# Fillers in the opening, weight splits moved to VectorE, adaLN columns in the up stage, and slack for TensorE's operands in the plan

## The chip, the cores and the metric

The kernel runs on one NeuronCore of a Trainium2 chip. The metric is the device time of one execution of the program in microseconds. The kernel before takes 800.14 us, the median of 3 runs (799.01, 800.98 and 800.14). One more execution was profiled; it took 800.93 us.

A NeuronCore has TensorE (matrix products, PE in the profile), VectorE (DVE), ScalarE (ACT), GpSimd (POOL) and SyncE (SP, which here only issues DMAs). Each has its own queue of instructions; they meet through semaphores. Matmuls read their operands from SBUF and write to PSUM banks.

## The reference, cut to what matters

One block of an encoder for a sequence of S = 512 with D = 1024, all in float32. Its parts, in the order of the reference:

```python
mod = silu(c) @ w_ada + b_ada                      # six vectors of 1024
h = rms_norm(x, norm1_g) * (1 + scale1) + shift1
qa, ka, va, qb, kb, vb, qi, ki, wi, gates = split(h @ w_in)   # 512 x (6 x 512 + 324 + 2048)
y_a = dsa_sparse_attention(rms_norm(qa), rms_norm(ka), va, qi, ki, wi)   # top 128 keys a query
y_b = differential_attention(rms_norm(qb), rms_norm(kb), vb, lam)        # two softmaxes, subtracted
merged = g_a * (y_a @ w_up_a) + g_b * (y_b @ w_up_b)          # g = sigmoid(gates)
x = x + gate1 * (merged @ w_o)
h2 = rms_norm(x, norm2_g) * (1 + scale2) + shift2
ff = (silu(h2 @ w_ff1) * (h2 @ w_ff3)) @ w_ff2                # inner width 2816
x = x + gate2 * ff
```

Both attentions are causal by chunks of 64 and have ALiBi distances; the sparse one scores keys with an indexer (qi, ki, wi) and keeps the 128 best.

## The kernel before, in words

**Precision.** Every float32 operand of a matmul is written as a high and a low half in the type fp32r: ScalarE casts (`whi<-raw`, line 429), and VectorE (`wlo<-raw,whi`, line 453) or GpSimd (the same name, line 501) subtracts the cast from the value. A product is three matmuls, high by high, high by low and low by high, summed in a PSUM bank (`three`, line 516 in the trace). The subtraction is called a split below. The set `ON_DVE` names the kinds of weights whose split VectorE does; before, these are the first eight blocks and the feed-forward part's, and GpSimd does the rest.

**Weights.** They come in blocks ("units") of 128 x 1024, half a megabyte each, in the order in which the stages need them: eight blocks `p` (indexer and branch b's q and k), two blocks a quad of heads (`qb0`, `kb1` and so on), 16 gate units `g0` to `g15`, 8 up units `u0` to `u7`, 8 blocks of the output projection w_o (called `o`, tiles `wo`), then the feed-forward blocks. There are four raw buffers and three buffers each for the halves. SyncE issues the loads in the planned order, and an issue waits for a free raw buffer. The adaLN matrices use the same raw buffers: a column unit of the second norm (`ada_col(1, j)`) is two transfers of `adat`, two column sums of 128 x 1024 on VectorE (line 473, shown as CUSTOM_DVE_ANT_0 and a short read of the accumulator; an ISA row in the order) and two small operations for `acol` and `hcol`. A row of a residual gate (`ada_row`) is one transfer of `adar` and one multiply-add of 128 x 1024 on VectorE (line 467).

**Stages.** The opening loads x, sums its squares, takes the root on GpSimd (`rpow`, line 482), scales the four tiles of x (set `XS`: on ScalarE; the others on VectorE), and transposes 128 columns at a time. Per block of 128 channels it needs two column sums for the first norm; ScalarE then scales and shifts the transposed tile (line 438), casts it (`hh`), and VectorE makes the low half (`hl`). For the first block this is done in four pieces. Six matmuls on ready data (`idle`, line 805) whose result nobody reads stand ahead of the first transposes. From about 62 us on come the indexer's scores (`sc`), the search for the best keys (MAX8 and MATCH_REPLACE8, `select`), the quads with their normalization (`qn`, `qkT`, `qk`), the heads A0 to A7 and B0 to B3 (`S`, `PT`, `PV`), the gates between them, the eight up units (a product with the sigmoid of a gate for either branch, their sum, and the cast and split `mh`, `ml`), the output projection with the residual, the second norm, and from 440 us on the feed-forward part.

**What sets the order.** Operations are not issued where they are written. A class `Order` records each with its engine, an estimated cost, its buffers, and a priority: its number in the recording, shifted where the code stands in `moved(d)` (a negative shift is earlier). `plan` then runs a list scheduler over all engines: at each point in planned time an engine takes, of the operations whose inputs are done, the one with the lowest priority that has its buffers. An input is done at the planned end of its maker plus a latency from the table `HOPS`, by pair of engines. The order so found is the program, and each engine then works through its queue in that order, with the real times. The string `PROG` gives the recording's order between opening and output projection: quads and heads by name, `s8` eight rounds of the search, `g` and `u` the units, and `l2` two of the late adaLN items, eight rows and then eight column units of the second norm. Weight blocks are recorded ahead of their use with a shift of −250.

## Time and profile before

| | |
|---|---|
| time, median of 3 runs | 800.14 us |
| profiled execution | 800.93 us |
| its span, first to last instruction | 799.1 us |
| mean granted clock of TensorE | 0.996 |
| busy share PE, DVE, ACT, POOL | 98%, 57%, 44%, 25% |
| read from HBM | 95.16 MB |

The profile shows one execution. The span is its time from the first to the last instruction; 1.8 us lie around it. Busy time counts an engine's work without waiting, issuing or branching. A row of a timeline gives start, duration, engine, line, operation, the tiles written and read, and in brackets how long the engine stood idle before, and what ended that. [...] Matmuls overlap, so a row's duration is longer than its distance to the next one.

### The profile page before, as it was taken

What the parts mean: (1) busy time and instruction counts of PE and PEld (TensorE: products, weight loads), DVE (VectorE), ACT (ScalarE), POOL (GpSimd) and SP (SyncE); (2) the same over time, 40 slices, a digit from 0 to 9 for tenths busy, and PEclk for the clock granted to TensorE, in tenths of its full rate; (3) what the DMA queues carried; (4) which work ended last, traced back from release to release, by engine and by line L of the source; (5) the groups of instructions that cost most, each with busy time, mean ns of one, the idle gap of its engine ahead of it and who ended that gap; (6) DMA issues with size and microseconds to landing.
All of it is one profiled execution on the core that took longest, in us unless ns stands there. A gap on an engine that the chain in (4) does not pass through costs nothing.

```text
span 799.1 us, 11091 instructions
## 1 busy us (share of the span) xinstructions
PE 781.9 (98%) x4261; PEld 673.9 (84%) x4261; DVE 456.2 (57%) x898; ACT 350.1 (44%) x649; POOL 200.3 (25%) x129
## 2 busy tenths in 40 slices
...
GB/s 348 398 136 53 81 69 65 80 80 65 83 107 117 106 55 87 149 185 279 168 237 80 80 106 112 129 154 153 138 105 85 101 106 84 100 106 85 126 40 66
DMA packets 29147, 97.97 MB, mean 123 GB/s; under 512 B 3235, under 2 KB 4771, under 8 KB 29094
## 3 DMA queue, kind: packets, MB, share of 16 engines
...
q14 instruction: 20, 0.16, 0.1%
HBM read 95.16 MB, written 2.10 MB: 122 GB/s over the span
## 4 chain that ended last, share of the span: by engine, by line
PE 85%; DVE 7%; issue 3%; DMA 2%; ACT 2%; POOL 1%; SPq 0%; POOLq 0%; ACTq 0%; DVEq 0%
PE ff L516 44%; PE gate L516 11%; PE up L516 5%; PE wo L516 3%; PE kb L516 3%; PE qa L516 3%; PE ka L516 2%; PE S L516 2%; PE PT L529 2%; PE qb L516 2%; PE idx L516 2%; PE PVa L516 1%; PE va L516 1%; PE vb L516 1%; DMA raw<-in_wun 1%
## 5 line engine op out<-in xcount | busy, mean ns | idle before, releaser
L429 ACT CAST whi<-raw 128x1024 fp32r<-128x1024 f32 x109 | 114.6, 1052 | 292.3 <-PE ff L516 148.2
L501 POOL TENSOR_TENSOR wlo<-raw,whi 128x1024 fp32r<-128x1024 f32 x46 | 114.9, 2499 | 157.9 <-ACT whi L429 133.3
L453 DVE TENSOR_TENSOR wlo<-raw,whi 128x1024 fp32r<-128x1024 f32 x63 | 77.1, 1225 | 117.4 <-ACT whi L429 114.6
L516 PE MATMUL ff<-h2l,whi 128*128 128x512 f32 (+1 forms) x384 | 142.5, 371 | 0.0
L516 PE MATMUL ff<-h2h,wlo 128*128 128x512 f32 (+1 forms) x384 | 142.4, 371 | 0.0
L516 PE MATMUL ff<-h2h,whi 128*128 128x512 f32 (+1 forms) x384 | 142.3, 372 | 0.0
L516 PE MATMUL ff<-whi,f 128*128 128x512 f32 (+1 forms) x310 | 95.1, 385 | 0.0
L516 PEld LDWEIGHTS ff<-h2l,whi 128*128 128x128 f32 x384 | 72.3, 188 | 12.5
L516 PEld LDWEIGHTS ff<-h2h,wlo 128*128 128x128 f32 x384 | 72.2, 188 | 12.5
L516 PEld LDWEIGHTS ff<-h2h,whi 128*128 128x128 f32 x384 | 72.2, 188 | 12.5
L516 PEld LDWEIGHTS ff<-whi,f 128*128 128x128 f32 x310 | 58.0, 188 | 11.6
L516 PE MATMUL ff<-wlo,f 128*128 128x512 f32 (+1 forms) x155 | 59.5, 385 | 0.0
L459 DVE TENSOR_TENSOR silu<-ff,silu 128x512 f32<-128x512 f32 x22 | 15.2, 692 | 69.4 <-PE ff L516 69.4
L516 PE MATMUL gate<-hh,whi 128*128 128x512 f32 x128 | 51.4, 402 | 0.0
L516 PE MATMUL gate<-hh,wlo 128*128 128x512 f32 x128 | 51.1, 401 | 0.0
L516 PE MATMUL gate<-hl,whi 128*128 128x512 f32 x128 | 51.0, 399 | 0.0
L473 DVE CUSTOM_DVE_ANT_0 raw<-raw,cs 128x1024 f32<-128x1024 f32 x32 | 45.7, 1440 | 4.2 <-DMA raw<-in_adat 2.7
L438 ACT ACTIVATE sx<-sx,nm 128x128 f32<-128x128 f32 (+3 forms) x64 | 35.7, 560 | 9.7 <-DVE nm L473 9.4
L482 POOL TENSOR_TENSOR r<-v,mhalf 128x16 f32<-128x16 f32 (+2 forms) x14 | 27.9, 1993 | 43.9 <-DVE v L463 40.3
L516 PEld LDWEIGHTS ff<-wlo,f 128*128 128x128 f32 x155 | 29.1, 188 | 5.9
L467 DVE SCALAR_TENSOR_TENSOR acc<-raw,csc,acc 128x1024 f32<-128x1024 f32 x16 | 20.7, 1294 | 22.0 <-DMA raw<-in_adar 21.9
L516 PE MATMUL wo<-wo,mh 128*128 128x512 f32 x96 | 30.2, 393 | 1.3 <-ACT mh L429 1.3
...
## 6 DMA issues: line engine op xcount, KB each, us to landing
raw<-in_wun SPq DMA_DIRECT2D x118, 512.0 KB, 3.3
raw<-in_adat SPq DMA_DIRECT2D x32, 512.0 KB, 7.3
raw<-in_adar SPq DMA_DIRECT2D x16, 512.0 KB, 3.3
x<-in_x SPq DMA_DIRECT2D x4, 512.0 KB, 5.9
...
xr<-in_x SPq DMA_DIRECT2D x4, 512.0 KB, 5.8
...
```

What stands on the lines that cost most here:

```text
L429: nc.scalar.copy(g(o), g(i))
L438: nc.scalar.activation(g(o), g(i), f, scale=g(scale), **kw)
L453: dve(n, False, lambda: nc.vector.tensor_sub(g(o), g(i), g(j)), (i, j), (o,), two=(i, j))
L459: dve(n, False, lambda: nc.vector.tensor_mul(g(o), g(i), g(j)), (i, j), (o,), two=(i, j))
L467: dve(n, False, lambda: nc.vector.scalar_tensor_tensor(g(o), g(i), g(s), g(j), op0=op0, op1=op1), (i, s, j), (o,), len(refs(s)), (i, j))
L473: dve(n, False, lambda: nc.vector.tensor_tensor_reduce(g(o), g(i), g(j), scale, init, op0, op1, g(acc)), (i, j), (o, acc), two=(i, j))
L482: G.op("POOL", 300 + 165 * m, lambda: nc.gpsimd.tensor_tensor(g(o), g(i), g(mhalf[:, 0:1].spread([P, m])), op=ALU.pow), refs(i, mhalf), re ...
L501: G.op("POOL", 147 + 2.106 * n, lambda: nc.gpsimd.tensor_sub(g(o.r()), g(i), g(hi)), (i, hi), (o,), port=True)
L516: lambda: nc.tensor.matmul(g(ap), g(lhsT.r()), g(rhs.r()), start=i == 0, stop=i == self.count - 1), refs(lhsT, rhs), (ap,))
L529: G.op("PE", 109, lambda: nc.tensor.transpose(g(ap), g(in_), g(idt)), refs(in_, idt), (ap,))
```

## The change

There are five edits. (1) The opening has thirteen idle matmuls instead of six. They use a bank of the transposes' pool (`tb`) and stand 60 places later in priority, so that the plan puts them where TensorE has nothing else; they are recorded at a planned cost of 500 instead of 700. Tile 0 of x goes to ScalarE too (`XS`), and the small activation `csc` has to wait for the last cast of the first block's pieces. (2) VectorE instead of GpSimd splits the output projection's blocks, the up units, and seven of the gate units. (3) The second norm's column units leave the list behind `l` and get a letter of their own, `k`; `PROG` spreads the rows from the u0 stage on and one column unit at a time from g7 to u5. (4) `l2` items stand later: none is left between the heads. (5) The plan adds 300 ns to the latency from ScalarE, VectorE or GpSimd to TensorE, so that a matmul counts as ready that much later.

```diff
@@ -37,7 +37,7 @@
 
 
 PROG = """scores s8 g0 qb1 vb0 B1 vb1 B0 g3 qa0 g13 g12 kb1 ka0 s9 s8 s9 B2 va0 s99 s8 qa1 g10 B3 g8 ka1 A2 A0 A3 va1
-A1 l2 A4 A6 l2 g2 g9 g5 A5 l2 A7 u0 g1 l2 u1 g11 g14 g7 g15 u2 u3 l2 l2 g4 g6 l2 u4 u5 u6 u7 l99"""
+A1 A4 A6 g2 g9 g5 A5 A7 u0 l2 g1 u1 l2 g11 g14 l2 g7 k1 l2 g15 k1 u2 k1 u3 k1 g4 k1 g6 k1 u4 k1 u5 k1 u6 u7 l99 k99"""
 PROG = PROG.split()
 
 
@@ -145,13 +145,14 @@
 
 
 W_MOVE, L_MOVE, S_MOVE = 250, -200, -100
-ON_DVE = ('f1', 'f3', 'f2', 'p')
+ON_DVE = ('f1', 'f3', 'f2', 'p', 'o', 'up') + tuple(('g', j) for j in (1, 11, 14, 7, 15, 4, 6))
 NRAW, NW, NT = 4, 3, 36
 DMA_LAG = 2000.0
+PE_SLACK = 300.0
 FS = 2
 DUP_POOL = ('kb0', 'kb1', 'ka0')
 HA = 4, 4, 4, 1
-XS = (1, 2)
+XS = (0, 1, 2)
 ADA_TAG = "pt"
 PC, XE, IB, H_MOVE, GT = 4, 4, 8, 40, 1
 LA = 2
@@ -358,6 +359,8 @@
                 n += 1
                 for d in pick.then:
                     x = pick.end + self.HOPS.get((e, d.eng), self.HOP)
+                    if d.eng == "PE" and e in ("ACT", "DVE", "POOL"):
+                        x += PE_SLACK
                     if x > d.ready:
                         d.ready, d.last = x, pick
                     d.need -= 1
@@ -423,7 +426,7 @@
     def refs(*xs):
         return [x for x in xs if isinstance(x, Ref)]
 
-    def act(o, i, n, f=AF.Copy, bias=None, scale=1.0, accum=None, also=()):
+    def act(o, i, n, f=AF.Copy, bias=None, scale=1.0, accum=None, also=(), after=()):
         def fn():
             if f == AF.Copy and bias is None and not isinstance(scale, Ref) and scale == 1.0:
                 nc.scalar.copy(g(o), g(i))
@@ -439,7 +442,7 @@
         table = f if f in (AF.Exp, AF.Sigmoid, AF.Silu) else None
         k, psum = len(refs(bias, scale, accum)), isinstance(i.v, Bank)
         op = G.op("ACT", (52 if psum else 94) + 0.833 * n + 93 * k, fn, refs(i, bias, scale), refs(o, accum), also=also,
-                  after=exps if f == AF.Sigmoid else (), table=table)
+                  after=exps if f == AF.Sigmoid else after, table=table)
         if f == AF.Exp:
             exps.append(op)
         return op
@@ -492,7 +495,7 @@
         return r
 
     def cp(o, i, n):
-        act(o.r(), i, n)
+        return act(o.r(), i, n)
 
     def sb(o, i, hi, n):
         sub(o.r(), i, hi, n)
@@ -659,8 +662,9 @@
             c = slice(p * n, p * n + n)
             act(f[:, c].k(p), b[:, c].k(p), n, AF.Identity, bias=one(hcol, cb), scale=one(acol, cb))
             h, l = (x[:, cb, c].k((0, p) if cb == 0 else cb) for x in (hh, hl))
-            cp(h, f[:, c].k(p), n)
+            cast = cp(h, f[:, c].k(p), n)
             sb(l, f[:, c].k(p), h, n)
+        return cast
 
     def stat_mm(bank, w, k, c=None, m=128, n0=0, n1=512, key=None):
         c = k * P if c is None else c
@@ -793,19 +797,20 @@
             dma(cst, a["cst"], 266)
             dma(lamv, a["lam"][0].partition_broadcast(P), 128)
             make_gains()
-            act(csc, vec[:, V_CC:V_CC + 8], 8, AF.Silu)
+            act(csc, vec[:, V_CC:V_CC + 8], 8, AF.Silu, after=(cast,))
         w = take(("p", cb))
         if cb == 0:
             scale_x(NB - 1)
         with G.moved(-H_MOVE if cb else 0):
-            make_h(cb)
+            cast = make_h(cb) if cb == 0 else (make_h(cb), cast)[1]
         if cb == 0:
-            idle = Bank("idle")
-            for _ in range(6):
-                G.op("PE", 700, lambda: nc.tensor.matmul(g(idle[:, 0:256]), g(cs[:, 0:P]), g(cs[:, 0:256]), start=True, stop=True),
-                     (cs,), (idle,))
             bi = [Bank("idx", x) for x in ("sb", "sb", "tb")]
             bq, bk = [Bank("qb0"), Bank("qb0")], [Bank("kb0"), Bank("kb0")]
+            idle = Bank("idle", "tb")
+            with G.moved(60):
+                for _ in range(13):
+                    G.op("PE", 500, lambda: nc.tensor.matmul(g(idle[:, 0:256]), g(cs[:, 0:P]), g(cs[:, 0:256]), start=True, stop=True),
+                         (cs,), (idle,))
         def index_mm():
             stat_mm(bi[2], w, cb, c=256, m=68, key=324)
             stat_mm(bi[0], w, cb, c=0, n0=128, key=324)
@@ -1069,7 +1074,7 @@
                     else:
                         select_end(i)
 
-    late = [("r", 0, k) for k in range(8)] + [("c", 1, cb) for cb in range(8)]
+    late, late2 = [("r", 0, k) for k in range(8)], [("c", 1, cb) for cb in range(8)]
     last = [("r", 1, k) for k in range(8)]
 
     def ada_late(n):
@@ -1081,6 +1086,12 @@
                         ada_col(1, j)
                     else:
                         ada_row(s, j)
+
+    def ada_cols(n):
+        for _ in range(n):
+            if late2:
+                with G.moved(L_MOVE):
+                    ada_col(1, late2.pop(0)[2])
 
     ohl = {}
     onum = [0]
@@ -1102,7 +1113,7 @@
             tag = "pt" if i < 4 else ("sx" if i < 7 else "t")
             hi, lo = pair(tag, "wo")
             cp(hi, t[:, kk * 512:kk * 512 + 512], 512)
-            psub(lo, t[:, kk * 512:kk * 512 + 512], hi, 512)
+            (sb if "o" in ON_DVE else psub)(lo, t[:, kk * 512:kk * 512 + 512], hi, 512)
             ohl[2 * k + kk, h] = (hi, lo)
 
     for w in PROG:
@@ -1112,7 +1123,7 @@
             for i in range(1, NB):
                 scores(i)
         else:
-            {"s": select, "A": head_a, "B": head_b, "g": gate, "u": up, "l": ada_late}[w[0]](int(w[1:]))
+            {"s": select, "A": head_a, "B": head_b, "g": gate, "u": up, "l": ada_late, "k": ada_cols}[w[0]](int(w[1:]))
 
 
     ahead(UIX[("o", 3, 1)] + 1)
```

The first place is the start of TensorE's queue. `cs` is the broadcast of the conditioning vector, `xT` are the transposes of x, `qb` and `kb` the first matmuls with a weight. Before, it stands like this:

```order
L601 MATMUL cs<-crow,ones 128x512 x2
L805 MATMUL idle<-cs 128x256 x6
L529 MATMUL xT<-vec,x 128x128 x6
L516 MATMUL qb_204<-whi,hh 128x256
L516 MATMUL qb_204<-wlo,hh 128x256
```

And after the change:

```order
L604 MATMUL cs<-crow,ones 128x512 x2
L812 MATMUL idle<-cs 128x256 x8
L532 MATMUL xT<-vec,x 128x128
L812 MATMUL idle<-cs 128x256 x2
L532 MATMUL xT<-vec,x 128x128
L812 MATMUL idle<-cs 128x256
L532 MATMUL xT<-vec,x 128x128
L812 MATMUL idle<-cs 128x256
L532 MATMUL xT<-vec,x 128x128
L812 MATMUL idle<-cs 128x256
L532 MATMUL xT<-vec,x 128x128 x4
L519 MATMUL qb_217<-whi,hh 128x256
```

Eight idle matmuls stand in a row and five between the first transposes.

The second place is VectorE's queue where the first score tile of the search (`sc`) is summed and the first quads are normalized (`qn`) and stacked (`qk`), with the numbers of the tiles. The old queue has here:

```order
L463 TENSOR_SCALAR sc_784<-relu_772,wi_770 128x256
L467 SCALAR_TENSOR_TENSOR sc_784<-relu_778,wi_770,sc_784 128x256
L467 SCALAR_TENSOR_TENSOR sc_784<-relu_793,wi_770,sc_784 128x256
L459 TENSOR_TENSOR qn_811<-kb0_207,r_762 128x512
L453 TENSOR_TENSOR qk_798<-qkT_781,qk_798 64x512
L453 TENSOR_TENSOR qk_804<-qkT_781,qk_804 64x512
L459 TENSOR_TENSOR qn_840<-kb0_235,r_762 128x512
L467 SCALAR_TENSOR_TENSOR sc_784<-relu_813,wi_770,sc_784 128x256
L866 MEMSET sc_784 64x64
L872 MAX m8_868<-sc_784 128x8
L453 TENSOR_TENSOR qk_850<-qkT_835,qk_850 64x512
L453 TENSOR_TENSOR qk_862<-qkT_835,qk_862 64x512
```

The new one, from the second multiply-add on:

```order
L470 SCALAR_TENSOR_TENSOR sc_798<-relu_806,wi_784,sc_798 128x256
L470 SCALAR_TENSOR_TENSOR sc_798<-relu_812,wi_784,sc_798 128x256
L462 TENSOR_TENSOR qn_828<-kb0_221,r_779 128x512
L456 TENSOR_TENSOR qk_816<-qkT_800,qk_816 64x512
L456 TENSOR_TENSOR qk_825<-qkT_800,qk_825 64x512
L871 MEMSET sc_798 64x64
L877 MAX m8_855<-sc_798 128x8
L878 MATCH_REPLACE sc_798<-m8_855,sc_798 128x256
L462 TENSOR_TENSOR qn_871<-kb0_260,r_779 128x512
L877 MAX m8_884<-sc_798 128x8
L878 MATCH_REPLACE sc_798<-m8_884,sc_798 128x256
L456 TENSOR_TENSOR qk_876<-qkT_857,qk_876 64x512
```

The third multiply-add has moved ahead of the first `qn` of kb, and the search's first two rounds stand ahead of the second pair of `qk` subtractions.

The third place is VectorE's queue at the end of the up stage, where the product of unit 5 and its successors (`gate`), and the output projection's operand (`ml`) are made. Before:

```order
L459 TENSOR_TENSOR gate<-up,gate 128x512 x3
L453 TENSOR_TENSOR ml<-gate,mh 128x512
L459 TENSOR_TENSOR gate<-up,gate 128x512
L456 TENSOR_TENSOR gate<-gate 128x512
L459 TENSOR_TENSOR gate<-up,gate 128x512
L453 TENSOR_TENSOR ml<-gate,mh 128x512
L456 TENSOR_TENSOR gate<-gate 128x512
L453 TENSOR_TENSOR ml<-gate,mh 128x512
L456 TENSOR_TENSOR gate<-gate 128x512
```

And after, from the product of unit 6 on:

```order
L462 TENSOR_TENSOR gate<-up,gate 128x512 x2
L456 TENSOR_TENSOR wlo<-raw,whi 128x1024
L456 TENSOR_TENSOR wo<-raw,wo 128x512 x5
L456 TENSOR_TENSOR ml<-gate,mh 128x512
L456 TENSOR_TENSOR wo<-raw,wo 128x512
L459 TENSOR_TENSOR gate<-gate 128x512
L456 TENSOR_TENSOR wo<-raw,wo 128x512 x6
L456 TENSOR_TENSOR ml<-gate,mh 128x512
L462 TENSOR_TENSOR gate<-up,gate 128x512 x2
L456 TENSOR_TENSOR wlo<-raw,whi 128x1024
L459 TENSOR_TENSOR gate<-gate 128x512
L456 TENSOR_TENSOR ml<-gate,mh 128x512
```

The twelve halves of w_o and two splits of 1024 columns stand between the products of the last two units; the column sums, of which the old queue still had four behind this place, all stand ahead of it.

## Rows read from the trace of the kernel before

**Rows 1.** The head of the page: span, then busy time of each engine, its share of the span and its instructions.

```profile
span 799.1 us, 11091 instructions
...
PE 781.9 (98%) x4261; PEld 673.9 (84%) x4261; DVE 456.2 (57%) x898; ACT 350.1 (44%) x649; POOL 200.3 (25%) x129
```

**Rows 2.** Busy time by stretch: the stretch in us from the span's start and its length, then busy us and instructions of PE, PEld, DVE, ACT and POOL, the granted clock, the DMA engines' share and GB/s.

```profile
62.00:108.00 46.00, 43.13 (x322) 40.37 (x322) 44.28 (x124) 27.18 (x57) 25.45 (x17) 1.00 0.20 70
108.00:310.00 202.00, 200.91 (x1369) 182.84 (x1368) 152.69 (x396) 135.15 (x311) 105.98 (x71) 1.00 0.25 84
310.00:378.00 68.00, 68.00 (x303) 56.35 (x302) 39.60 (x60) 26.00 (x36) 29.33 (x13) 1.00 0.53 181
378.00:395.00 17.00, 14.20 (x60) 10.51 (x58) 11.90 (x11) 9.39 (x17) 15.84 (x10) 1.00 0.56 185
395.00:440.00 45.00, 44.45 (x236) 37.87 (x237) 32.27 (x56) 20.88 (x51) 11.55 (x10) 1.00 0.47 160
440.00:799.00 359.00, 355.33 (x1650) 297.49 (x1648) 130.83 (x145) 94.15 (x116) 0.00 (x0) 1.00 0.31 104
```

**Rows 3.** The same view for two pieces of the opening.

```profile
11.33:14.74 3.41, 1.14 (x7) 0.58 (x6) 2.55 (x8) 1.75 (x3) 1.63 (x1) 1.00 1.04 408
14.74:21.57 6.83, 5.62 (x25) 5.52 (x26) 6.77 (x16) 5.21 (x14) 0.00 (x0) 0.50 1.04 401
```

**Rows 4.** Timeline of TensorE in the opening. The trace counts the six idle matmuls as twelve passes.

```profile
6.25 5.35 PE L805 MATMUL idle<-cs 128*128 128x256 f32 x12
...
15.95 0.58 PE L516 MATMUL qb<-whi,hh 128*128 128x256 f32 x1 [1.32 <-ACT hh L429]
...
18.04 0.41 PE L516 MATMUL qb<-wlo,hh 128*128 128x256 f32 x1
18.25 0.41 PE L516 MATMUL qb<-whi,hl 128*128 128x256 f32 x1
...
24.30 0.28 PE L516 MATMUL qb<-whi,hh 128*128 128x256 f32 x1
24.42 0.28 PE L516 MATMUL qb<-wlo,hh 128*128 128x256 f32 x1
```

**Rows 5.** Timelines of GpSimd, VectorE and ScalarE in the opening: the root, the last step of the first block's shift, the first scaled and shifted piece, and the low half of the second block.

```profile
11.27 1.68 POOL L482 TENSOR_TENSOR r<-v,mhalf 128x2 f32<-128x2 f32 x1 [3.08 <-DVE bs L463]
...
13.67 0.15 DVE L456 TENSOR_TENSOR hcol<-mcol,vec 128x1 f32<-128x1 f32 x1
...
14.92 0.80 ACT L438 ACTIVATE xT<-xT,hcol,acol 128x128 f32<-128x128 f32 x2
...
21.96 0.68 DVE L453 TENSOR_TENSOR hl<-xT,hh 128x512 fp32r<-128x512 f32 x1
```

**Rows 6.** Timelines of TensorE, VectorE and GpSimd around 70 us.

```profile
72.78 0.63 PE L529 MATMUL qkT<-vec,qn 128*128 128x128 f32 x4 [1.76 <-DVE qk L453]
...
68.10 2.46 DVE L467 SCALAR_TENSOR_TENSOR sc<-relu,wi,sc 128x256 f32<-128x256 f32 x1
...
70.78 0.43 DVE L872 MAX8 m<-sc 128x8 f32<-128x256 f32 x1
71.24 1.39 DVE L453 TENSOR_TENSOR qk<-qkT,qk 64x512 fp32r<-64x512 f32 x2
...
67.88 2.40 POOL L501 TENSOR_TENSOR wlo<-raw,whi 128x1024 fp32r<-128x1024 f32 x1 [0.31 <-ACT whi L429]
```

**Rows 7.** Waits of TensorE from 62 to 310 us: what waited, for what, and then us in total, times, longest.

```profile
PE S L516 <- DVE nm L473: 0.9, 2, 0.5
```

**Rows 8.** Groups of instructions over the whole span: count, busy us and mean ns of one, and the idle time before them.

```profile
L501 POOL TENSOR_TENSOR wlo<-raw,whi 128x1024 fp32r<-128x1024 f32 x46 | 114.9, 2499 | 157.9 <-ACT whi L429 133.3
L453 DVE TENSOR_TENSOR wlo<-raw,whi 128x1024 fp32r<-128x1024 f32 x63 | 77.1, 1225 | 117.4 <-ACT whi L429 114.6
...
L473 DVE CUSTOM_DVE_ANT_0 raw<-raw,cs 128x1024 f32<-128x1024 f32 x32 | 45.7, 1440 | 4.2 <-DMA raw<-in_adat 2.7
...
L501 POOL TENSOR_TENSOR wo<-raw,wo 128x512 fp32r<-128x512 f32 x12 | 19.4, 1644 | 1.2 <-ACT wo L429 1.2
```

**Rows 9.** Timeline of TensorE at the start of the output projection.

```profile
384.75 0.50 PE L516 MATMUL wo<-wlo,mh 128*128 128x512 f32 x1 [1.37 <-POOL wlo L501]
...
389.25 0.73 PE L516 MATMUL wo<-wo,mh 128*128 128x512 f32 x2 [1.25 <-ACT mh L429]
```

**Rows 10.** Timelines of VectorE and GpSimd in the up stage: a product and the column sums behind it, and a split of GpSimd's.

```profile
341.04 0.69 DVE L459 TENSOR_TENSOR gate<-up,gate 128x512 f32<-128x512 f32 x1 [17.26 <-PE up L516]
341.64 1.22 DVE L473 CUSTOM_DVE_ANT_0 raw<-raw,cs 128x1024 f32<-128x1024 f32 x1
...
355.58 2.58 POOL L501 TENSOR_TENSOR wlo<-raw,whi 128x1024 fp32r<-128x1024 f32 x1 [2.72 <-ACT whi L429]
...
356.38 2.87 DVE L473 CUSTOM_DVE_ANT_0 raw<-raw,cs 128x1024 f32<-128x1024 f32 x1 [0.47 <-issue]
...
359.18 1.22 DVE L473 CUSTOM_DVE_ANT_0 raw<-raw,cs 128x1024 f32<-128x1024 f32 x1
360.32 0.08 DVE L473 DVE_READ_ACCUMULATOR2_ANT mcol<- 128x1 f32 x1
360.32 0.21 DVE L467 SCALAR_TENSOR_TENSOR acol<-mcol,bs,vec 128x1 f32<-128x1 f32 x1
```

**Rows 11.** DMA issues from 310 to 400 us: count, KB each, median us from issue to landing.

```profile
raw<-in_wun SPq DMA_DIRECT2D x16, 512.0 KB, 3.9
```

## The prediction

> **What bounds the kernel now.** I read the page's head first, then the busy time of each engine stage by stage, then the opening microsecond by microsecond, then TensorE's waits, and last the groups of VectorE and GpSimd. [...] First, TensorE works 781.9 of 799.1 us [rows 1], so only its idle time, its slow clock and the tail after its last matmul can be won. Second, the stretch from 440 us on holds nothing: the feed-forward part is one unbroken row of matmuls, and the 3.67 us that TensorE lacks there (359.00 − 355.33 [rows 2]) are the output's last steps, which the change leaves alone. Third, the losses sit in four places [rows 2]: 62 to 108 us (46.00 − 43.13 = 2.87 idle), 108 to 310 us (202.00 − 200.91 = 1.09), 378 to 395 us (17.00 − 14.20 = 2.80) and 395 to 440 us (0.55). [...]
>
> **The opening.** Before, the six idle matmuls run back to back from 6.25 us and are over at 11.6; the first real matmul starts at 15.95 [rows 4]. The change has thirteen, five of them between the first transposes, each of which waits for its scaled tile of x; so the engine is idle in short pieces, not in one long one. If the clock then stays at its upper level, every 256-column matmul after 15.95 starts 0.12 us after the one before it (24.30 to 24.42) and not 0.21 (18.04 to 18.25) [rows 4]: 5.62 busy us become 5.62 × 0.12/0.21 = 3.2, a gain of 2.4. Not all of it arrives. VectorE now scales the last x tile between the two column sums of the first unit and not behind them, and that waits for GpSimd's root, which ended at 12.95 [rows 5]; I shift the root by −0.25 for the tile that ScalarE now scales, and find scale end 13.4, second sum 14.6, hcol about 15.0 instead of 13.8 [rows 5]. ScalarE's transposed piece started at 14.92 behind its casts before, now at 15.1: the start slips by 0.2. And the second unit's low half (hl), which came at 21.96 + 0.68 = 22.64 [rows 5], still comes at about 22.9, since four pieces of the first unit's are now done behind one more sum; TensorE at full clock is there at about 22.4. So 2.4 − 0.2 − 0.5 = 1.7, and I take 1.5. Ends: 2.4, and −0.3 where the clock falls all the same and only the later start is left. The seven added matmuls cost nothing so long as the last is over before the first real one; eight in a row from 6.25 end near 12.4, the other five fill waits. ScalarE's later csc has no reader before the rows of the first gate.
>
> [...]
>
> **62 to 108 us.** The longest wait is 1.76 us before a transposition (qkT) that needs a PSUM bank [rows 6]. The bank is freed by two subtractions at 71.24 that stand behind a 2.46 us multiply-add, which ended as GpSimd's split (67.88 + 2.40) did [rows 6]; the operation itself takes 0.5. In the new order all three multiply-adds of that sum stand in front of kb's normalization, ahead of GpSimd's second split, and two search rounds stand in front of the subtractions. Walking the queue from 63.2 us with the row's durations I get 71.1 for the freed bank instead of 72.6. Gain 1.5; I take 1.2, since the new place also hangs on a ScalarE cast that moved back by one relu. Ends: 1.8 (the wait is gone), and −1.0 (two more max and match pairs, some 0.5 us each, with nothing hidden).
>
> **108 to 310 us.** The slack of 300 ns in the plan moves a matmul whose operand comes from another engine behind other ready work. It takes no work away. Visible is 1.09 of idle time [rows 2], of it 0.9 for score tiles waiting on VectorE since 62 us [rows 7]; a matmul is drawn 0.28 long where the next starts 0.12 later [rows 4], so waits under 0.16 leave no idle time. Also, six of the eight row sums leave the heads' stage and four splits of 1.22 come in, so VectorE has less to do there. I take 1.0. Ends: 3.3 (the hidden waits twice as large as the visible), −1.5 (other operands come late instead).
>
> **310 to 395 us.** This is where splits go from GpSimd to VectorE. Seventeen of 1024 columns leave GpSimd at 2.50 us and twelve of 512 at 1.64 us, 62 us in all; they cost VectorE 1.225 each and, as its product of the same size does, 0.69: 29 us [rows 8, 10]. What goes: waits of TensorE of 2.80 us [rows 2], of which two are 1.37 and 1.25, the first of them on a GpSimd split of wo [rows 9]. Also a stall of VectorE itself: its column sum of 356.38 took 2.87 us beside a GpSimd split that ended at 358.16, the next one 1.22 [rows 10]; with nothing of GpSimd's left after the heads, all take 1.22. What comes: VectorE had 39.60 of 68 us busy from 310 to 378 [rows 2] and now does, between the product of up unit 2 and that of up unit 6, fourteen column sums, seven 1024-wide subtractions and seventeen 512-wide operations. By full durations (a column sum with its read is 1.22 + 0.08, and each second one is followed by two small operations of 0.21 and 0.15 [rows 5, 10]) that is 14 × 1.30 + 7 × 1.22 + 17 × 0.69 + 7 × 0.36 = 41 us; back to back they overlap by some 0.08 each (359.18 + 1.22 is 0.08 past 360.32 [rows 10]), which over 52 operations gives some 36.5. TensorE's 160 matmuls there last 160 × 68.00/303 = 36 us [rows 2]. So VectorE is full, but not past it. Behind the product of unit 6 the new queue holds two 1024-wide subtractions, the twelve of wo, and seven 512-wide gate operations up to the last operand: 2.4 + 8.2 + 4.8 = 15.4 us, and then ScalarE has one cast to do. TensorE has 24 matmuls of unit 7 and 45 of wo before it needs that operand: 69 × 0.224 = 15.5. I put 1.5 us of waits in place of 2.80. Gain 1.3. Ends: 2.8, and −5.3 (third rival). The loads keep up: with four raw buffers, 3.9 us from issue to landing [rows 11] and 1.2 for the split, a block can come every 1.3 us, a little more with ScalarE's cast, against three blocks in two units' worth of matmuls of 5.4 us each at most.
>
> **395 to 440 us.** The last two columns of the second norm were summed here; they are now done before. Of 0.55 us I take 0.3; ends 0.55 and −0.5.
>
> **Sum.** 1.5 + 1.2 + 1.0 + 1.3 + 0.3 = 5.3 us. The profiled execution took 800.93 us, 1.83 around a span of 799.1; 800.93 − 5.3 = 795.6. It lies 0.8 above the median of the three runs, 800.14; against that the forecast is 794.8.
>
> **Rivals.**
> *The clock falls all the same* (chance 0.12). For it: the fillers are 256 columns wide and stand between waits that only the run sets. Against it: in the profile the clock rose to 1.00 after the same matmuls had run back to back from 6.25, and it fell only after a stretch with 1.14 of 3.41 us busy [rows 3, 4]. The opening then gives −0.3 instead of 1.5: 796.6.
> *The plan's slack only shuffles* (0.18). The waits at 70 us and in the heads are replaced by others; for it speaks that the order of nearly every engine from 60 to 310 us changes, against it that each named wait has its cause in a queue place that moves. Without 1.2 and 1.0: 797.0.
> *VectorE becomes the bound of the up stage* (0.12), the case that ends slower. Place: the start of wo. VectorE's queue is served in order: at 341.04 its product waited for TensorE for 17.26 us with a column sum right behind it, which ran at once afterwards [rows 10]. If operations don't overlap (41 us instead of 36.5) and the column sums keep their mean of 1.44 [rows 8] in place of 1.30 (14 × 0.14 = 2.0), VectorE is 6.6 us late when wo begins, and TensorE waits 8.1 us where it waited 2.8. Then −5.3 there against 4.0 elsewhere: 801.4. It decides from a wait of 6.8 us on at wo. Against it: the mean of 1.44 contains the stretched ones beside GpSimd [rows 10], which the change removes. [...]
>
> **How the numbers follow.** The forecast has 0.58; its own range is 792 to 797.5. A difference under 0.3% (2.4 us) can't be told from none here: below 797.7 is faster, above 802.5 slower. Faster: nearly all of 0.58 (0.56), most of the clock's 0.12 (0.10), 0.11 of the shuffle's 0.18: 0.77. Slower: 0.05 of the third rival and as much for its worse ends and for several ends together: 0.10. The rest, 0.13, is no change. The range for 8 in 10 reaches down to 790 (the upper ends of the opening and of 310 to 395 and half that of the heads) and up to 800 (the shuffle and half of the third rival).
>
> **What would show it.** Opening: granted clock 1.00 from 11 us on, the first unit's matmuls 0.12 apart, the last idx matmul of the eighth unit about 1.5 us earlier. At 70 us: no wait above 0.5 on qkT. From 310 us on: GpSimd empty but for the four roots, column sums of 1.22, VectorE at nine tenths and more, the sum of TensorE's waits between 375 and 395 us near 1.5. From 440 us: the same matmuls, 5 us earlier. I am wrong if the clock shows 0.50 after 14 us, if TensorE waits more than 2.8 us at wo, or if the stretch from 108 to 310 us is longer than before.

## The result

The changed kernel takes 805.99 us (median of 4 runs, 805.43 to 806.72), the kernel before 800.56 beside it. The ratio is 1.0071 with a 95% interval of 1.0053 to 1.0089: the change makes the kernel slower by 5.7 us, where 5.3 us less were forecast. The profiled execution took 806.12 us with a span of 804.3.

The head of its page, which answers to [rows 1]:

```profile
span 804.3 us, 11105 instructions
...
PE 784.8 (98%) x4275; PEld 676.0 (84%) x4275; DVE 469.8 (58%) x926; ACT 350.4 (44%) x650; POOL 137.3 (17%) x100
```

TensorE has 2.9 us more of work, about what the seven added idle matmuls take, and the span is 5.2 longer. GpSimd has lost 63 us, as counted. The busy time of all engines by stretch, with the columns of [rows 2, 3]:

```profile
11.33:14.74 3.41, 3.41 (x17) 2.84 (x16) 2.82 (x4) 1.89 (x4) 1.63 (x1) 1.00 1.03 401
14.74:21.57 6.83, 6.59 (x44) 5.22 (x43) 6.83 (x21) 5.60 (x16) 0.00 (x0) 1.00 1.04 403
62.00:108.00 46.00, 40.49 (x304) 37.97 (x304) 44.95 (x117) 25.08 (x49) 22.68 (x16) 1.00 0.21 70
108.00:310.00 202.00, 200.50 (x1375) 182.85 (x1375) 150.82 (x396) 134.43 (x312) 96.29 (x68) 1.00 0.21 69
310.00:350.00 40.00, 37.79 (x168) 30.90 (x168) 30.37 (x41) 17.56 (x26) 0.00 (x0) 1.00 0.68 228
350.00:402.00 52.00, 49.02 (x202) 39.92 (x201) 44.53 (x77) 20.40 (x31) 0.00 (x0) 0.93 0.80 273
402.00:440.00 38.00, 38.00 (x190) 31.88 (x190) 20.44 (x36) 18.92 (x48) 2.73 (x3) 1.00 0.19 65
```

The opening did what was forecast: the granted clock, a share of TensorE's full one, stays at 1.00 where it was 0.50 from 14.74 to 21.57 us [rows 3]. Everything lost is at two places. From 62 to 108 us TensorE stands idle for 5.51 us where it was 2.87, and from 310 to 402 us for 2.21 + 2.98 where it was 2.80, at a mean clock of 0.93 in the last stretch. The waits behind that (what waited, for what; us in total, times, longest):

```profile
PE score L519 <- ACT relu L441: 4.2, 2, 2.3
PE wo L519 <- ACT mh L432: 3.0, 1, 3.0
...
PE acc L519 <- DVE accl L456: 2.2, 1, 2.2
PE S L519 <- DVE nm L476: 1.2, 2, 0.8
```

Of the waits of [rows 6, 7, 9] the one on qkT is down to 0.2 and those on GpSimd at wo are gone; none of the three that stand first here was in the trace of before at this length.

Idle time misses gaps that are shorter than the overlap of two matmuls, and a slow clock. For a table over all kernels I therefore added up, for each matmul, its distance to the next start less the usual distance (0.227 us for 512 columns, 0.174 for 384, 0.119 for 256, 0.060 for 128, 0.109 for a transposition, 0.212 for a pass of a filler). This lost time by stretch, from one profile each, in us:

| kernel | ratio to before, 95% | 58-108 | 108-310 | 310-372 | 372-405 | 405-450 |
|---|---|---|---|---|---|---|
| before | | 5.8 | 9.1 | 0.1 | 3.9 | 1.1 |
| the change | 1.0071 (1.0053-1.0089) | 8.7 | 8.5 | 4.3 | 4.8 | 0.7 |
| e1 opening only | 0.9969 (0.9957-0.9981) | 5.5 | 9.3 | 0.0 | 3.4 | 1.0 |
| e2 change, splits on GpSimd | 1.0092 (1.0076-1.0108) | 7.5 | 8.9 | 2.7 | 9.1 | 0.5 |
| e3 change, old rows and columns | 1.0033 (1.0020-1.0045) | 7.0 | 8.4 | 0.0 | 7.1 | 0.8 |
| e4 change, no slack | 1.0040 (1.0025-1.0054) | 5.5 | 9.2 | 2.9 | 7.3 | 1.4 |
| e5 change, small transfers | 0.9967 (0.9951-0.9984) | 8.6 | 8.6 | 0.1 | 1.4 | 0.8 |
| e6 change, short sums | 0.9988 (0.9975-1.0002) | 7.1 | 8.6 | 1.3 | 1.3 | 0.8 |
| e7 opening + splits | 1.0022 (1.0010-1.0033) | 5.5 | 9.4 | 0.1 | 6.8 | 1.4 |
| e8 opening + columns | 1.0073 (1.0057-1.0089) | 5.8 | 9.3 | 5.1 | 6.8 | 1.3 |
| e9 early columns | 1.0095 (1.0073-1.0118) | 5.5 | 16.2 | 6.6 | 1.8 | 1.4 |
| e10 early columns, GpSimd | 1.0116 (1.0095-1.0136) | 5.8 | 17.6 | 8.5 | 0.0 | 1.3 |
| e11 change, no stall | 1.0006 (0.9992-1.0020) | 4.1 | 8.7 | 1.7 | 9.3 | 0.7 |
| e12 opening, no fillers | 0.9995 (0.9983-1.0008) | 5.8 | 9.2 | 0.0 | 4.3 | 1.0 |
| e13 change, five buffers | 1.0094 (1.0081-1.0107) | 7.5 | 8.1 | 5.1 | 5.9 | 0.7 |
| e14 opening + three splits | 0.9962 (0.9950-0.9974) | 4.6 | 9.3 | 0.0 | 4.8 | 1.0 |
| e15 the same, five buffers | 0.9987 (0.9978-0.9995) | 4.2 | 11.7 | 0.1 | 2.5 | 1.7 |
| e16 change + three splits | 1.0020 (1.0003-1.0037) | 5.3 | 8.8 | 1.4 | 3.6 | 0.8 |
| e17 e14 + two wo splits | 0.9980 (0.9968-0.9992) | 4.3 | 9.3 | 0.0 | 5.2 | 1.7 |
| e18 e17 + two up splits | 1.0000 (0.9990-1.0010) | 4.2 | 9.4 | 0.0 | 6.9 | 1.2 |

Each row is one execution: those of e3, e6, e13, e15 and e16 were the shortest of their runs (e16: 798.98 us, its median 802.52), those of e9, e10, e11 and e14 the longest (e11: 803.91, its median 800.56), so the ratios tell what an edit is worth and the rows only where.

For the change against before this is −0.6 from 108 to 310 us, +2.9 ahead of it, +5.1 from 310 to 405 and −0.4 behind; ahead of 58 us the loss falls from 11.1 to 6.4, of which the seven fillers use 3.0 (14 passes of 0.212). The sum is 5.3, and the last matmul ends 5.2 us later.

### The profile page after: what moved, and what is told of

Read it like the earlier page. It is cut to its first block, busy times and chain, and to the rows that moved or that the text cites. A ratio compares the mean times of both kernels' runs of the same rounds, so it can differ in the third digit from the quotient of the medians.

```text
span 804.3 us, 11105 instructions
## 1 busy us (share of the span) xinstructions
PE 784.8 (98%) x4275; PEld 676.0 (84%) x4275; DVE 469.8 (58%) x926; ACT 350.4 (44%) x650; POOL 137.3 (17%) x100
## 4 chain that ended last, share of the span: by engine, by line
PE 79%; DVE 11%; DMA 5%; ACT 3%; issue 1%; POOL 0%; SPq 0%; DVEq 0%; POOLq 0%; ACTq 0%
PE ff L519 44%; PE gate L519 8%; PE wo L519 5%; PE qa L519 3%; PE kb L519 3%; PE ka L519 2%; DMA raw<-in_adat 2%; PE S L519 2%; PE up L519 2%; PE va L519 2%; PE PT L532 2%; PE idx L519 2%; DVE sc L878 1%; DVE m L877 1%; PE qb L519 1%; DVE sc L470 1%
## 5 line engine op out<-in xcount | busy, mean ns | idle before, releaser
L456 DVE TENSOR_TENSOR wlo<-raw,whi 128x1024 fp32r<-128x1024 f32 x80 | 97.8, 1224 | 118.4 <-ACT whi L432 115.7
L504 POOL TENSOR_TENSOR wlo<-raw,whi 128x1024 fp32r<-128x1024 f32 x29 | 69.6, 2400 | 85.2 <-ACT whi L432 82.3
L519 PEld LDWEIGHTS ff<-whi,f 128*128 128x128 f32 x310 | 57.9, 188 | 11.7
L476 DVE CUSTOM_DVE_ANT_0 raw<-raw,cs 128x1024 f32<-128x1024 f32 x32 | 38.8, 1220 | 7.1 <-DMA raw<-in_adat 7.1
```

What stands on the lines that cost most here:

```text
L456: dve(n, False, lambda: nc.vector.tensor_sub(g(o), g(i), g(j)), (i, j), (o,), two=(i, j))
L476: dve(n, False, lambda: nc.vector.tensor_tensor_reduce(g(o), g(i), g(j), scale, init, op0, op1, g(acc)), (i, j), (o, acc), two=(i, j))
L504: G.op("POOL", 147 + 2.106 * n, lambda: nc.gpsimd.tensor_sub(g(o.r()), g(i), g(hi)), (i, hi), (o,), port=True)
L519: lambda: nc.tensor.matmul(g(ap), g(lhsT.r()), g(rhs.r()), start=i == 0, stop=i == self.count - 1), refs(lhsT, rhs), (ap,))
```

## The experiments

### The change taken apart

In the diffs below `...` marks what is left out. Edit 1 alone, on the kernel before (e1):

```diff
-XS = (1, 2)
+XS = (0, 1, 2)
...
-            idle = Bank("idle")
-            for _ in range(6):
+            idle = Bank("idle", "tb")
+            with G.moved(60):
+                for _ in range(13):
```

> The kernel before with edit 1 alone (thirteen idle matmuls, tile 0 of x on ScalarE, the later csc). Theory: the opening is the part that worked; in the changed kernel the last idx matmul of the eighth block ends 1.55 us earlier (56.45 against 58.0) at a granted clock of 1.00, so this kernel takes about 799.0 us against 800.5, and the rest of it is the kernel before. Rival: the gain is lost again at the first later wait (the qkT wait near 70 us hangs on VectorE and GpSimd, not on TensorE), then 800.3 to 800.8.

798.77 us, ratio 0.9969. The opening's gain arrives: about 2.5 us.

The same with six fillers in the old bank, so that only the scaling and the later csc are new (e12, against e1):

```diff
-            idle = Bank("idle", "tb")
-            with G.moved(60):
-                for _ in range(13):
+            idle = Bank("idle")
+            for _ in range(6):
```

> The opening's edit without its fillers: six idle matmuls in their old bank as before, tile 0 of x on ScalarE and the later csc as in the change, all else as before. Theory (fillers keep the clock up): the granted clock is 0.50 again for some 6 us after about 15 us, 800.5 to 801.3 us. Rival (scaling and csc brought the gain): 798.5 to 799.5 us.

0.9995, no difference from before. Its opening and, under it, that of the run with fillers (stretch and length, busy time of the five engines, clock, DMA share, GB/s):

```profile
11.33:14.74 3.41, 1.30 (x6) 0.64 (x6) 2.82 (x7) 1.97 (x3) 1.41 (x1) 1.00 1.02 397
14.74:21.57 6.83, 5.56 (x31) 5.21 (x32) 6.83 (x19) 5.59 (x16) 0.00 (x0) 0.75 1.04 404
```

```profile
11.33:14.74 3.41, 3.41 (x18) 2.87 (x17) 2.82 (x6) 1.90 (x4) 1.51 (x1) 1.00 1.03 405
14.74:21.57 6.83, 6.35 (x42) 5.00 (x41) 6.83 (x21) 5.58 (x16) 0.00 (x0) 1.00 1.04 403
```

With 1.30 of 3.41 us busy the clock fell behind it, to a mean of 0.75; with the fillers, at 3.41 of 3.41, it stayed at 1.00. So by the medians the fillers are worth 0.9995 − 0.9969, about 2.1 us, and what the scaling is worth can't be told from nothing (0.9983 to 1.0008). The two profiled executions show only a part of this in the opening: the last idx matmul of the eighth block ends at 56.00 us with the fillers and at 56.95 without (58.00 before, where the same stretch had a clock of 0.50 and not 0.75); another 0.9 us lies at wo (3.4 us lost against 4.3).

The change without edit 2 (e2), without edits 3 and 4 (e3), and without edit 5 (e4):

```diff
-ON_DVE = ('f1', 'f3', 'f2', 'p', 'o', 'up') + tuple(('g', j) for j in (1, 11, 14, 7, 15, 4, 6))
+ON_DVE = ('f1', 'f3', 'f2', 'p')
```

> The changed kernel with the splits of w_o, of the up units and of the seven gate units back on GpSimd. Theory (the ten additional half-megabyte transfers between 310 and 395 us, on four raw buffers, are what is late): the waits of 2.2 us at acc and of 3.0 us at wo stay or shrink little, 805 to 807 us. Rival (VectorE is the bound of the up stage): both waits go, with the fall of the clock behind each of them, 801 us or less.

```diff
-late, late2 = [("r", 0, k) for k in range(8)], [("c", 1, cb) for cb in range(8)]
+late, late2 = [("r", 0, k) for k in range(8)] + [("c", 1, cb) for cb in range(8)], []
```

with the old string `PROG`:

> The changed kernel with the old order of rows and column units (edits 3 and 4 undone): eight rows between the heads again, four of the column sums behind the start of wo. Theory: the acc wait leaves the up stage, the loads keep up, the stretch from 310 to 395 us is again at 3 us of lost time or under instead of 9; 800 to 801.5 us. Rival (VectorE's splits are the bound): the wait at wo stays above 2.5 us, 803 us or more.

```diff
-PE_SLACK = 300.0
+PE_SLACK = 0.0
```

> The changed kernel without the 300 ns in the plan. By the orders, the move of the third multiply-add at 62 us and of the search rounds comes from this edit alone. Theory: the score waits of 1.8 and 2.3 us near 65 and 79 us go and the qkT wait of 1.8 us is back, so 62 to 108 us loses 2.9 us as before instead of 5.5: 803.4 us. Rival: the slack saves as much in the heads as it costs at 62 us, then 805 to 807 us.

808.78, 804.69 and 804.43 us. So within the change rows and columns cost 0.38% (3 us) and the slack 0.31% (2.5 us); whether the splits on VectorE help there can't be told (1.0092 against 1.0071, and the intervals overlap). None of the three runs comes near 800. In e2 the waits stayed, as its theory said, at a longer time; e3 came out by its rival, for without the late columns 7.1 us are lost at wo all the same, now on `DVE ml`; e4 lies between its two. Two more runs give edits 2 and 3 with 4 singly, on top of the opening (e7, e8; the diffs are against the change):

```diff
-PE_SLACK = 300.0
+PE_SLACK = 0.0
...
-late, late2 = [("r", 0, k) for k in range(8)], [("c", 1, cb) for cb in range(8)]
+late, late2 = [("r", 0, k) for k in range(8)] + [("c", 1, cb) for cb in range(8)], []
```

with the old `PROG`:

> The kernel before with edits 1 and 2 (opening, splits on VectorE), the old order of rows and columns, no slack. Theory: with the old order four column sums stand in VectorE's queue ahead of a low half ml that TensorE needs, as in the run without the late columns, where that wait was 2.7 us; 801.5 to 803.5 us. Rival (the splits alone do no harm, and only slack and late columns do): 798 to 799.5 us.

```diff
-PE_SLACK = 300.0
+PE_SLACK = 0.0
...
-ON_DVE = ('f1', 'f3', 'f2', 'p', 'o', 'up') + tuple(('g', j) for j in (1, 11, 14, 7, 15, 4, 6))
+ON_DVE = ('f1', 'f3', 'f2', 'p')
```

> The kernel before with edits 1, 3 and 4 (opening, late rows and columns), splits on GpSimd as before, no slack. Theory: loads come late and VectorE's sums are stretched beside GpSimd's splits, so this is the worst of the family without slack: 805 to 808 us. Rival (columns alone are harmless while GpSimd does the splits): 798 to 800 us.

1.0022 and 1.0073. From the opening's 0.9969 the splits alone cost 0.53% (4.2 us), the late rows and columns alone 1.04% (8.3 us), and both together (e4) 0.71% (5.7 us): each is harmful, and the splits repair part of what the columns do. In the first of the two, TensorE at wo:

```profile
386.30 0.50 PE L519 MATMUL wo<-wo,ml 128*128 128x512 f32 x1 [2.27 <-DVE ml L456]
...
395.46 0.73 PE L519 MATMUL wo<-wo,ml 128*128 128x512 f32 x2 [0.96 <-DVE ml L456]
```

and VectorE, which makes that ml at 385.56 behind six splits of w_o, and the last one behind four column sums, two of which wait for their transfers:

```profile
383.75 1.90 DVE L456 TENSOR_TENSOR wo<-raw,wo 128x512 fp32r<-128x512 f32 x3 [0.22 <-ACT wo L432]
385.56 0.68 DVE L456 TENSOR_TENSOR ml<-gate,mh 128x512 fp32r<-128x512 f32 x1
...
393.37 1.23 DVE L476 CUSTOM_DVE_ANT_0 raw<-raw,cs 128x1024 f32<-128x1024 f32 x1 [0.99 <-DMA raw<-in_adat]
```

### Around 70 us

In the changed kernel VectorE's three multiply-adds of the first score, TensorE's wait and GpSimd's split beside them are:

```profile
62.07 4.33 DVE L470 SCALAR_TENSOR_TENSOR sc<-relu,wi,sc 128x256 f32<-128x256 f32 x3
...
78.41 2.76 DVE L470 SCALAR_TENSOR_TENSOR sc<-relu,wi,sc 128x384 f32<-128x384 f32 x1
```

```profile
67.03 0.61 PE L519 MATMUL score<-ki,qi 128*128 128x384 f32 x2 [1.83 <-ACT relu L441]
```

```profile
63.13 2.39 POOL L504 TENSOR_TENSOR wlo<-raw,whi 128x1024 fp32r<-128x1024 f32 x1
...
78.39 2.37 POOL L504 TENSOR_TENSOR wlo<-raw,whi 128x1024 fp32r<-128x1024 f32 x1 [2.73 <-DVE sc L466]
```

The split runs to 65.52, and all multiply-adds are done at 66.40; at 78.4 the same happens again. ScalarE's relu waits 2.05 us for the sum, TensorE 1.83 for the relu's bank. To see whether the stall or the order does it, GpSimd's three splits of this stretch were replaced in the same order by clearing the tile, which leaves out the low half of these weights (e11):

```diff
+        if u in (("qb1", 1), ("vb0", 0), ("vb0", 1)):
+            G.op("POOL", 147 + 2.106 * n, lambda: nc.gpsimd.memset(g(lo[:, :n]), 0.0), (t, hi), (lo,), port=True)
+            splits[u] = (hi, lo)
+            return
```

> The changed kernel in its own order, but GpSimd's splits of the second block of qb1 and of both blocks of vb0 are replaced by clearing the tile (the low half of these weights is left out). Theory (the slack put the score's multiply-adds beside GpSimd's split, and an operation of VectorE with two operands in SBUF stands until that split is over): the three multiply-adds from 62.07 us on take 1.6 instead of 4.33 us, the score waits of 1.8 and 2.3 us fall below 0.6 each; 802.5 to 804 us. Rival (the search rounds that now stand ahead of the subtractions are what is late): 805 to 807 us.

1.0006 against 1.0071, 5 us less than the change. The multiply-adds now take:

```profile
62.31 1.66 DVE L470 SCALAR_TENSOR_TENSOR sc<-relu,wi,sc 128x256 f32<-128x256 f32 x3
```

and TensorE's idle time from 62 to 108 us is 1.16 instead of 5.51. The order of every engine is the same and the stall is gone, so the stall is the cause; in the changed kernel TensorE waits for none of these low halves, so it isn't their earlier arrival that helps.

In two close pairs the one that started second, by hundredths of a microsecond, was held. At 78.4 us the split started 0.02 us ahead of the multiply-add, which then took 2.76. In the run e6 below, which has the change's order, the multiply-add started 0.07 us ahead of the split; it took 0.61, the split 2.79, and the second score wait didn't come:

```profile
79.02 0.61 DVE L470 SCALAR_TENSOR_TENSOR sc<-relu,wi,sc 128x384 f32<-128x384 f32 x1
...
79.09 2.79 POOL L504 TENSOR_TENSOR wlo<-raw,whi 128x1024 fp32r<-128x1024 f32 x1 [2.72 <-DVE sc L882]
```

The start alone does not settle it in every case: of the three multiply-adds at 62.07 us in the changed kernel the second was held, 3.15 us long against 0.48, and it is recorded from 62.66 on, 0.47 us ahead of the split.

A version that can be used does these three splits on VectorE, first with the opening alone (e14), then with the whole change (e16):

```diff
-ON_DVE = ('f1', 'f3', 'f2', 'p')
+ON_DVE = ('f1', 'f3', 'f2', 'p', ('qb1', 1), ('vb0', 0), ('vb0', 1))
```

> The opening's edit alone, plus the splits of the second block of qb1 and of both blocks of vb0 on VectorE instead of GpSimd. Theory (a split on VectorE costs 1.22 us there, on GpSimd it can hold VectorE for up to 2.4): the qkT wait of 1.7 us near 70 us goes, 60 to 80 us loses 1.5 us instead of 3.6; 796 to 797.5 us. Rival (VectorE is busy for 44 of 46 us there, so three more operations in its queue cost what they save): 798.5 to 800 us.

> The whole change with the same three splits on VectorE as well. Theory (the stall beside GpSimd is what the slack ran into): 62 to 108 us loses 2 to 3 us instead of 5.5, 802.5 to 804 us; the up stage is as late as in the change. Rival (VectorE full around 70 us): 805.5 to 807 us.

0.9962 and 1.0020. With the change it gives back 4 us, as its theory said. With the opening alone the loss from 58 to 108 us falls from 5.5 to 4.6, but the wait at wo on GpSimd is then 2.6 us. Of the kernels that leave nothing out it has the lowest ratio, but it can't be told from e1's 0.9969.

### The up stage

What stands behind the acc wait in the changed kernel is VectorE's queue at 345 us; the row of PE is from TensorE's timeline:

```profile
345.68 1.23 DVE L476 CUSTOM_DVE_ANT_0 raw<-raw,cs 128x1024 f32<-128x1024 f32 x1 [1.67 <-DMA raw<-in_adat]
346.83 0.69 DVE L462 TENSOR_TENSOR gate<-up,gate 128x512 f32<-128x512 f32 x1
347.44 1.22 DVE L456 TENSOR_TENSOR accl<-acc,acch 128x1024 fp32r<-128x1024 f32 x1
```

```profile
348.70 0.74 PE L519 MATMUL acc<-accl,ones 128*128 128x512 f32 x2 [2.21 <-DVE accl L456]
```

ScalarE's acch was ready at 344.17, and accl needed 1.22 us; a column sum that waited 1.67 us for its transfer stood in front of it. From 310 to 395 us VectorE's waits and the DMA issues are:

```profile
DVE raw L476 <- DMA raw<-in_adat: 7.1, 10, 1.7
DVE acc L470 <- DMA raw<-in_adar: 2.8, 4, 1.4
...
DVE gate L462 <- PE up L519: 0.6, 1, 0.6
```

```profile
raw<-in_wun SPq DMA_DIRECT2D x19, 512.0 KB, 4.5
raw<-in_adat SPq DMA_DIRECT2D x16, 512.0 KB, 4.5
raw<-in_adar SPq DMA_DIRECT2D x5, 512.0 KB, 4.4
```

Before, VectorE's waits for TensorE and for adat in this stretch were:

```profile
DVE gate L459 <- PE up L516: 21.1, 5, 17.3
...
DVE raw L473 <- DMA raw<-in_adat: 2.7, 3, 1.4
```

Forty transfers in 85 us, one every 2.1 us, where it was 29, and 9.9 us in which the operation at the head of VectorE's queue waits for one of the adaLN's, where it was 2.7, with the weights' splits and the products behind it. For TensorE it waits 0.6 us instead of 21.1: it is hardly ever ahead. At wo ScalarE then has the cast of mh behind casts of w_o that wait for late loads:

```profile
390.25 1.14 ACT L432 CAST wo<-raw 128x512 fp32r<-128x512 f32 x2 [1.62 <-DMA raw<-in_wun]
392.03 1.14 ACT L432 CAST wo<-raw 128x512 fp32r<-128x512 f32 x2 [0.64 <-DMA raw<-in_wun]
393.07 0.61 ACT L432 CAST mh<-gate 128x512 fp32r<-128x512 f32 x1
```

```profile
393.74 1.17 PE L519 MATMUL wo<-wo,mh 128*128 128x512 f32 x3 [2.98 <-ACT mh L432]
```

Two runs keep the change's own order in every engine. One (e5) has the second norm's sixteen transfers bring 8 of 1024 columns, the sums run over a resident tile and keep their length; the other (e6) keeps the transfers and sums over 64 columns:

```diff
+            if s:
+                dma(w[:, 0:8], a["adat"][s][cb][i][:, 0:8], 512)
+                ttr(w, cs, cs, 1.0, 0.0, ALU.mult, ALU.add, one(mcol, 16 * s + 2 * cb + i), 1024)
+                continue
```

> The changed kernel in its own order, but each of the second norm's sixteen column transfers brings 8 of 1024 columns, and the sum runs over a tile that is already there (so the second norm's scale and shift come out other than the reference's); VectorE's sixteen sums keep their length and place. Theory (the loads are late in the up stage, ten more half megabytes on four raw buffers): the acc wait of 2.2 us and the wo wait of 3.0 us go, with the 1.6 and 1.7 us of slow clock behind them, 798 to 800 us. Rival (VectorE's queue of sums and splits is full): the wo wait stays at 2.5 us or more, 803 us or more.

```diff
+            if s:
+                dma(w, a["adat"][s][cb][i], 512)
+                ttr(w[:, 0:64], w[:, 0:64], cs[:, 0:64], 1.0, 0.0, ALU.mult, ALU.add, one(mcol, 16 * s + 2 * cb + i), 1024)
+                continue
```

> The changed kernel in its own order and with all its transfers, but each of the sixteen column sums runs over 64 of the 1024 columns (second norm's scale and shift differ from the reference's), which takes some 18 us off VectorE between 310 and 395 us and frees each raw buffer about 1.1 us earlier. Theory (loads): part of the waits stays, since the same bytes come in, 802 to 805 us. Rival (VectorE full): both waits go, 798 to 800 us.

797.59 and 799.49 us: 0.9967 and 0.9988. Either one takes the loss away (1.5 and 2.6 us from 310 to 405 instead of 9.1). The two stretches of 310 to 395 us, small transfers and then short sums:

```profile
310.00:395.00 85.00, 83.97 (x373) 69.03 (x372) 74.00 (x118) 37.96 (x56) 0.00 (x0) 1.00 0.53 173
```

```profile
310.00:395.00 85.00, 83.17 (x368) 68.23 (x367) 59.00 (x115) 36.49 (x53) 0.00 (x0) 1.00 0.80 270
```

With all transfers but short sums the DMA engines move 270 GB/s there, more than the change's 251 from 310 to 395 us, and TensorE hardly waits. So the transfers' rate alone was not the limit. With small transfers VectorE is busy for 74.00 us of 85 and TensorE hardly waits either, so VectorE's work alone was not it. Nor are its waits for transfers alone: with short sums they are even longer than in the change,

```profile
DVE raw L476 <- DMA raw<-in_adat: 14.6, 15, 1.9
DVE acc L470 <- DMA raw<-in_adar: 3.4, 4, 1.4
```

and cost TensorE next to nothing. Work and waits for adaLN transfers together are 70.14 + 9.9 = 80.0 us of 85 in the change, 74.00 + 2.8 = 76.8 with small transfers and 59.00 + 18.0 = 77.0 with short sums. Both theories had expected one of the two runs to keep its waits; the loss needs the two together. One form of that would be the turnover of the four raw buffers (e13):

```diff
-NRAW, NW, NT = 4, 3, 36
+NRAW, NW, NT = 5, 3, 35
```

> The changed kernel with five raw buffers instead of four (and 35 small tiles instead of 36, to make room). Theory (what makes the loads late is the turnover of the four buffers: landing, a wait in VectorE's queue, the sum, and only then the next issue): acc and wo wait under 1.2 us each, and the granted clock stays at 1.00; 799 to 801.5 us. Rival (the transfers themselves are at their rate, so another buffer only makes each landing longer): the waits stay above 2 us, 804 to 807 us.

1.0094: no faster than the change's 1.0071, and this theory falls in the form in which it was put. VectorE waited 8.1 us for adat and 0.5 for adar (7.1 and 2.8 in the change), and at wo TensorE waited:

```profile
389.68 0.76 PE L519 MATMUL wo<-whi,mh 128*128 128x512 f32 x1 [4.15 <-DVE gate L462]
```

TensorE needed a PSUM bank that a product of VectorE had to free, and that product (at 388.85) stood behind the twelve halves of w_o and two wide splits, which VectorE worked through without a gap from 377.94 us on. Five buffers with the opening and the three splits (e15, against e14) did no good either:

> The run before (opening's edit and three splits on VectorE) with five raw buffers and 35 small tiles. Theory (turnover of buffers makes the blocks of w_o late in this order too): the wo waits of about 2 us shrink to under 1, 1 to 1.5 us less than the run with four buffers. Rival (GpSimd's 19.7 us of splits of w_o are last there): no difference.

0.9987, above e14's 0.9962: the wo wait shrank to 1.7 us and 2.4 us more were lost in the heads.

A repair by moving the columns ahead was tried, with the splits on VectorE (e9) and on GpSimd (e10):

```diff
-... B2 va0 s99 s8 qa1 g10 B3 g8 ka1 A2 A0 A3 va1
-A1 l2 A4 A6 l2 g2 g9 g5 A5 l2 A7 u0 g1 l2 u1 g11 g14 g7 g15 u2 u3 l2 l2 g4 g6 l2 u4 u5 u6 u7 l99"""
+... B2 va0 s99 s8 k1 qa1 k1 g10 B3 k1 g8 k1 ka1 k1 A2 A0 l2 A3 va1
+A1 l2 A4 k1 A6 l2 g2 k1 g9 g5 A5 l2 A7 u0 k1 g1 u1 g11 g14 g7 g15 u2 u3 g4 g6 u4 u5 u6 u7 l99 k99"""
```

> Edits 1 and 2 (opening, splits on VectorE), no slack, the rows between the heads as before, and the second norm's eight column units moved ahead of and between the heads (from the quad qa1 on), so that none of their transfers is left in the up stage. Theory (loads are late in the up stage when adaLN transfers stand between the weights): from 310 to 440 us TensorE loses under 2 us, against 4.2 with the opening alone and 10.0 in the changed kernel; 796 to 797.5 us. Rival (VectorE has no room in the heads, and sums there delay operands of S and PT): the gain is eaten between 160 and 310 us, 799 to 802 us.

> As the run with early columns, but with the splits on GpSimd as in the kernel before. Theory: with the loads in time what is left at wo is GpSimd's own 19.7 us for the twelve halves of w_o, waits of about 2 us; 797.5 to 799 us, so the splits on VectorE are worth 1 to 2 us once the columns are out of the way. Rival (splits on VectorE are worth nothing): the same time as that run within 0.5 us.

1.0095 and 1.0116, slower than either theory allowed, and whether the splits make a difference here the two intervals don't tell. The place is that of the first rival: wo loses under 2 us as hoped, and the heads, of which the last now end at 327 and 330 us, lose 7 to 8 us more up to 310 and another 6.6 and 8.5 behind it, with waits such as

```profile
190.72 0.52 PE L532 MATMUL PT<-vec,sx 128*128 128x128 f32 x3 [1.85 <-DVE qk L470]
```

Last, the splits were moved in small steps, with the old columns: to e14 first the two wide splits of w_o (e17), then those of the last two up units (e18).

```diff
-ON_DVE = ('f1', 'f3', 'f2', 'p', ('qb1', 1), ('vb0', 0), ('vb0', 1))
+ON_DVE = ('f1', 'f3', 'f2', 'p', ('qb1', 1), ('vb0', 0), ('vb0', 1), ('o', 0, 0), ('o', 1, 0))
```

> The run with the opening and three splits, plus the two 1024-wide splits of w_o's first blocks on VectorE (the other twelve halves stay on GpSimd). Theory (at wo GpSimd's splits are last with the old columns, and VectorE has some 10 us free between 350 and 395 us): the wo wait of 2.6 us on GpSimd falls below 1 and the granted clock stays at 1.00, 796 to 797 us. Rival (VectorE's queue in order makes any split there hold up the low halves ml, as with all splits moved): 798 to 801 us.

```diff
-... ('o', 0, 0), ('o', 1, 0))
+... ('o', 0, 0), ('o', 1, 0), ('up', 6), ('up', 7))
```

> The same with the splits of the last two up units on VectorE as well. Theory (room on VectorE remains for two more): within 0.5 us of the run with two, or better, 795.5 to 797 us. Rival (the step from a few splits to many is where VectorE's queue becomes the last one): 798.5 to 801 us.

0.9980 and 1.0000, each worse than the one before it, against the theory and within what the rival said. In the first the wait at wo is as long as it was on GpSimd, but on mh:

```profile
385.83 1.20 PE L519 MATMUL wo<-wo,mh 128*128 128x512 f32 x2 [2.81 <-ACT mh L432]
```

## Why the prediction was wrong

**The opening** (1.5 us taken): right, with its mechanism. The last idx matmul of the eighth block ended at 58.00 us before and 56.45 after; alone the edit gives 2.5 us (0.19 to 0.43%). The rival by which the clock falls all the same did not happen in any profile with the fillers.

**62 to 108 us** (gain of 1.2 taken, loss of 2.9 measured): wrong. The step that failed is the walk along VectorE's queue. It saw that all three multiply-adds now stand ahead of GpSimd's second split, and not that they now meet the first: before, only the third met a split, and nothing waited for it but the second pair of subtractions. The walk starts at VectorE's first scaling of the score (63.20 us before) and frees the bank at 71.1, 7.9 us later (9.43 before). In the change the scaling stands at 61.62 and the bank is free at 72.48, 10.86 later; in e11, without the stall, it is 8.30 (61.87 and 70.17). So the rest of the walk was good to 0.4 us, and the stall is what it lacked. In the change two score waits of 1.8 and 2.3 us come of it. The qkT wait went, as forecast (0.2 us is left, and none in e11): without the stall the stretch loses 4.1 us, against 5.5 without the slack (e4), which is the gain that was taken. By the traces, the move of the third multiply-add comes from the slack: e2 and e3, which keep it, have the three in a row (4.32 us), e4, which doesn't, has them in the old places. The slack prices a hand-over to TensorE and moves everything behind it.

**108 to 310 us** (1.0): 0.6 by the distances, and the kernels with the slack lose 8.1 to 8.9 us here, those without 9.1 to 9.4 (e9, e10 and e15 aside). So the direction was right, but not by the waits that were named: the idle time went from 1.09 to 1.50 us and the wait for nm from 0.9 to 1.2, and the gain lies in gaps that leave no idle time. Of the rival that the slack only shuffles waits, the part at 70 us came true, and worse than it was priced; the part in the heads did not.

**310 to 395 us** (gain of 1.3 taken, loss of 5.1 measured): wrong, and the largest error. The step that failed is "the loads keep up". I reckoned three blocks in two units of 5.4 us, one in 3.6 us; in the changed kernel there is one transfer every 2.1 us, since six rows now come here as well and two transfers of a column unit stand between the blocks of weights. I took each column sum as 1.30 us with its read, and that was its length (1.22 without it, and no stretched one left), but left out that VectorE's queue stands until the transfer at its head is there, 9.9 us in all. The stretch of that sum, from the product of unit 2 to that of unit 6, shows it, here its row and then VectorE's wait in it:

```profile
341.34:383.44 42.10, 39.89 (x169) 32.49 (x168) 35.69 (x66) 13.39 (x17) 0.00 (x0) 0.96 0.78 268
```

```profile
DVE raw L476 <- DMA raw<-in_adat: 5.7, 8, 1.7
```

VectorE's work was 35.69 us, against 36.5 in the sum (36.8 by its own numbers, 41 − 52 × 0.08); the waits of 5.7 us, which the sum has at nothing, make the stretch 42.10 instead of 36. So VectorE, counted as just full, was late. At its end I left ScalarE "one cast to do", and took the loads of w_o to be there; the cast of mh stood behind casts that waited 1.62 and 0.64 us for theirs. The acc wait was not in my list at all. I credited the heads with six row sums that leave and charged them nowhere: they take 6 × 1.28 = 7.7 us from 313.7 us on, and the end of the rows, with its own cast, split and matmuls, moved from 322 us, where it cost no wait, to 345, among the column sums. No run put that split ahead of the column sum that held it.

**395 to 440 us** (0.3): 0.4 from 405 us on. Right.

**The rivals.** The third, with a chance of 0.12, had the direction, the stage and the order of VectorE's queue, but by its own condition, a wait of 6.8 us at wo, it did not come: there were 2.98 us, behind ScalarE's casts, and 2.21 at acc. Its 8.1 us came from longer sums (and 41 + 2.0 − 36 is 7.0, not 6.6); the sums were short. What I had named as the mark of being wrong, a wait of over 2.8 us at wo, is the wait of 2.98.

Taken together, 1.2 + 2.9 and 1.3 + 5.1 are 10.5 us, and the forecast of −5.3 becomes the +5.2 of the profile. The lateness of VectorE needs its work and its waits together, as e5 and e6 show. What stays open is why VectorE's waits with five buffers were hardly shorter, and why the small steps e17 and e18 move the wait at wo from GpSimd to ScalarE's casts with so little gain; the plan changes with each edit there, and none of these runs held the order fixed.
